# The rest of a quarter of the output weights: a negated copy and an accumulating DMA in place of a subtraction

## The chip, the cores and the metric

One core of one Trainium2 chip runs the kernel. The metric is the device time of one execution in microseconds (us); lower is better.

## What is computed

One layer of a hybrid decoder trunk for 256 tokens of width 4096, in float32. One input projection makes the columns of two head groups (a state-space group and a gated linear recurrence), each group works on its columns, and the two results of 4096 channels each go through one output projection, a residual and a LayerNorm:

```python
proj = x @ w_in                                  # 4096 x 18496
z, xbc, dt_raw, lx, lg = jnp.split(proj, ...)
...                                              # ssd_out and lru_out, 4096 channels each
mix = jnp.concatenate([ssd_out, lru_out], axis=-1)
res = DEEPNORM_ALPHA * x + mix @ w_out           # 8192 x 4096
out = (res - mean) * rsqrt(var + eps) * ln_g + ln_b
```

The change touches only the part `mix @ w_out`, and of the weights only how they are prepared.

## The kernel before, in words

**Three products for one.** Each float32 operand of a projection is split into a high part of 12 significant bits and the rest, both in the matmul's float32r type. The product is high x high + high x rest + rest x high, added up in PSUM.

**The order of the work.** The input projection of the recurrence (LRU) columns comes first, head by head; then the output projection of that half, whose result with alpha*x is spilled to DRAM; then the input projection of the state-space (SSD) columns; then the output projection of the SSD half, with the LayerNorm. All weights stream from DRAM once, in chunks of 128 partitions x 1024 float32 (512 KB).

**The function around the change** is `xstat` (L213 to L232). It makes 512 output columns for both blocks of 128 tokens. It runs over 16 chunks of weights; each chunk holds two of the 32 k-tiles. For a chunk it takes a `raw` tile (one of 4 buffers), loads it with a DMA from the SP queue (L219), calls `split` (L153), and issues 12 matmuls: for each of two k-tiles and two token blocks, high x high (L228), high x rest (L229) and rest x high (L230). `split` takes a `hi` and a `lo` tile (3 buffers each), and does two things:

```python
act.copy(hi, raw)                                # L160, ScalarE
dve.tensor_tensor(out=lo, in0=raw, in1=hi, op=ALU.subtract)   # L161, VectorE
```

So chunk n can be split only when the matmuls of chunk n-3 have let go of their `hi` and `lo`, and the load of chunk n+4 can start only when the split of chunk n has let go of its `raw`.

**Who calls `xstat`.** The output projection of the LRU half calls it 8 times with `src` the mixed activations `mix` (L423 on), the SSD input projection 8 times with `src` the layer's input `X` (the gate columns), and the output projection of the SSD half 7 times with `mix`. The last 512 columns of the SSD half are done by other code (L669 on) that calls `split` itself. The input projection's `wstat` also calls `split`.

**What else stands in the queues.** The elementwise work of a block is written as generators that `tick` advances once for each chunk (L231). In the LRU half, `gen_o1` (L364) loads `xa`, adds alpha*x and stores `spill`, all DMAs on the SP queue. During the last call there (r = 7), `dt_part` (L410) adds 32 matmuls (L419) of a narrow weight. The framework's scheduler then sets the final order on each engine, so instructions can stand earlier or later than they are written. GpSimd (POOL) has next to nothing to do: masks at the start, and small powers and fills (L534, L581, L587) later.

Of the kernel before, what the change touches and what calls it, by code (L numbers as in the profile page):

```python
"""Hybrid SSD / RG-LRU layer with DeepNorm post-norm on one Trainium2 core.

The two projections run on the tensor engine as float32 products made of three
passes: each operand is split exactly into a high part of 12 significant bits
and the rest, both in float32r, and high*high + high*rest + rest*high is
accumulated in float32 in PSUM.

Order: input projection of the LRU columns head by head, output projection of
the LRU half (spilled to DRAM with alpha*x), input projection of the SSD columns
group by group, output projection of the SSD half, LayerNorm.  The elementwise  # L10
work of a block is emitted between the weight chunks of the blocks after it.
"""
# [2 lines left out]

# [4 lines left out]
F32 = mybir.dt.float32  # L20
F32R = mybir.dt.float32r
I32 = mybir.dt.int32
AF = mybir.ActivationFunctionType
ALU = mybir.AluOpType

P = 128
# [5 lines left out]
LAG = 5  # L32
ON_ACT = ((2, 4, 6), (3, 6))
Z0, X0, B0, C0, DT0, LX0, LG0 = 0, 4096, 8192, 9216, 10240, 10304, 14400
# columns of the packed per-channel vectors
LCW, LCB, LBA, LBX, LLAM, SCW, SCB, SNW, MSK, NPK = 0, 128, 160, 192, 224, 256, 448, 496, 528, 534


def body(tc, xT, x, wb, wz, wd, wo, wg, pk, hv, ln_g, ln_b, out):
    nc = tc.nc  # L40
    act, dve, pe, pool, dma = nc.scalar, nc.vector, nc.tensor, nc.gpsimd, nc.sync.dma_start

    stack = contextlib.ExitStack()
    with stack:
        ent = stack.enter_context
        con = ent(tc.tile_pool(name="con", bufs=1))
# [4 lines left out]
        mp = ent(tc.tile_pool(name="mp", bufs=4, space=bass.MemoryType.PSUM))  # L51
        dram = ent(tc.tile_pool(name="dram", bufs=1, space=bass.MemoryType.DRAM))

# [1 line left out]
        pkt = con.tile([P, NPK], F32, name="pkt")  # L55
        hvt = con.tile([P, 3, 64], F32, name="hvt")
        ident = con.tile([P, P], F32, name="ident")
        mler = con.tile([P, P], F32R, name="mler")    # [k, l] = 1 where k <= l
        mgtr = con.tile([P, P], F32R, name="mgtr")    # [k, s] = 1 where k > s
        mle = mler.bitcast(F32)  # L60
        mhalf = con.tile([P, 2], F32, name="mhalf")
        c8 = con.tile([P, 32], F32, name="c8")
# [3 lines left out]
        adl = con.tile([P, 2, 64], F32R, name="adl")  # L66
        dec = con.tile([P, 64], F32, name="dec")
        ea = con.tile([P, 64], F32, name="ea")
        na = con.tile([P, 64], F32, name="na")        # exp(a_log)

        def load_consts():
            dma(pkt, pk)
# [16 lines left out]
            act.copy(mgtr, mgt)  # L89

        def exp_small(dst, src, n):
            """dst = exp(src) to float32 accuracy: 2^k * exp(r / 4)^4, zero below exp(-86.5)."""
            xc, k, r = t2k("ex", [P, n]), t2k("ek", [P, n]), t2k("er", [P, n])
            bits = t2k("eb", [P, n], I32)
            dve.tensor_scalar(xc, src, -87.0, 89.0, op0=ALU.max, op1=ALU.min)
            dve.tensor_scalar(k, xc, math.log2(math.e), 1.5 * 2.0 ** 23, op0=ALU.mult, op1=ALU.add)
            dve.tensor_scalar(k, k, 1.5 * 2.0 ** 23, None, op0=ALU.subtract)
            dve.scalar_tensor_tensor(out=r, in0=k, scalar=-0.693359375, in1=xc, op0=ALU.mult, op1=ALU.add)
            dve.scalar_tensor_tensor(out=r, in0=k, scalar=2.12194440054690583e-4, in1=r, op0=ALU.mult, op1=ALU.add)
            act.activation(r, r, AF.Exp, scale=0.25)  # L100
            yield
            dve.tensor_tensor(out=r, in0=r, in1=r, op=ALU.mult)
            dve.tensor_tensor(out=r, in0=r, in1=r, op=ALU.mult)
            dve.tensor_scalar(bits, k, 126.0, 2.0 ** 23, op0=ALU.add, op1=ALU.mult)
            dve.tensor_tensor(out=r, in0=r, in1=bits.bitcast(F32), op=ALU.mult)
            dve.tensor_scalar(xc, src, -86.5, 2.0, op0=ALU.is_ge, op1=ALU.mult)
            dve.tensor_tensor(out=dst, in0=r, in1=xc, op=ALU.mult)
            yield

        def softplus(dst, src, n, scale):  # L110
            """dst = softplus(scale * src), scale +1 or -1; relative accuracy for all sizes."""
            def t(nm):
                return t2k(nm, [P, n])
            ax, e, z, z2, q = t("ax"), t("e"), t("z"), t("z2"), t("q")
            dve.scalar_tensor_tensor(out=ax, in0=src, scalar=-1.0, in1=src, op0=ALU.mult, op1=ALU.min)
            yield from exp_small(e, ax, n)
            dve.tensor_scalar(z2, e, 2.0, None, op0=ALU.add)
            dve.reciprocal(z, z2)
            dve.tensor_tensor(out=z, in0=z, in1=e, op=ALU.mult)
            yield  # L120
            dve.tensor_tensor(out=z2, in0=z, in1=z, op=ALU.mult)
            dve.tensor_scalar(q, z2, 2.0 / 17, 2.0 / 15, op0=ALU.mult, op1=ALU.add)
            for k in (13, 11, 9, 7, 5, 3, 1):
                dve.tensor_tensor(out=q, in0=q, in1=z2, op=ALU.mult)
                dve.tensor_scalar(q, q, 2.0 / k, None, op0=ALU.add)
            dve.tensor_tensor(out=q, in0=q, in1=z, op=ALU.mult)
            dve.tensor_scalar(ax, src, scale, 0.0, op0=ALU.mult, op1=ALU.max)
            dve.tensor_tensor(out=dst, in0=ax, in1=q, op=ALU.add)
            yield

# [1 line left out]
        pend = []  # L132

        def tick():
# [18 lines left out]
        def split(raw, shape, extra=None):  # L153
# [7 lines left out]
            dve.tensor_tensor(out=lo, in0=raw, in1=hi.bitcast(F32), op=ALU.subtract)  # L161
            return hi, lo

        def rawtile(shape):
            return wp.tile(shape, F32, name="raw", tag="raw", bufs=4)

# [13 lines left out]
                              in1=X[:, k0:k0 + n, 0, :].bitcast(F32), op=ALU.subtract)  # L180

        def wstat(blocks, first=False):
            """Blocks of 256 columns of the input projection, by number, channel-major:
            one PSUM tile [128, 2, (high 256 | rest 256)] per block."""
            accs = [acc.tile([P, 2, 512], F32, name="acc") for _ in blocks]
            k0 = 0
            while k0 < KT:
# [23 lines left out]
            return accs  # L211

        def xstat(src, raws, before=None):  # L213
            """512 columns, sequence-major [128, 2 seq blocks, 512]; raws[chunk] is the DRAM of 2 k-tiles."""
            a = acc.tile([P, 2, 512], F32, name="acc")
            for ch in range(KT // 2):
                k0 = ch * 2
                raw = rawtile([P, 2, 512])
                dma(raw, raws[ch])  # L219
                hi, lo = split(raw, [P, 2, 512])  # L220
                if before is not None:
                    before(k0)
                for k in range(2):
                    kt = k0 + k
                    for sb in range(2):
                        sh = src[:, kt, 0, sb * P:(sb + 1) * P]
                        sl = src[:, kt, 1, sb * P:(sb + 1) * P]
                        pe.matmul(a[:, sb, :], lhsT=sh, rhs=hi[:, k, :], start=(kt == 0), stop=False)  # L228
                        pe.matmul(a[:, sb, :], lhsT=sh, rhs=lo[:, k, :], start=False, stop=False)  # L229
                        pe.matmul(a[:, sb, :], lhsT=sl, rhs=hi[:, k, :], start=False, stop=(kt == KT - 1))  # L230
                tick()  # L231
            return a  # L232
# [9 lines left out]
            return u  # L242

        def conv(u, wbase, bbase, stride, chans):
            """causal conv of width 4 along the free axis; yields between the two tiles."""
            y = t2k("cv")
            for c in range(2):
                ct = chans[c]
# [11 lines left out]
                yield  # L260
            return y

# [1 line left out]
        lgs = {}  # L264

        def gen_lg(h, a):
# [68 lines left out]

        ready = []

# [1 line left out]
        def gen_pre():  # L339
            load_consts()  # L340
            make_masks()
# [16 lines left out]
                a = wstat([lxc])[0]  # L358
            last = start(gen_lx(h, a))

# [1 line left out]
        spill = dram.tile([8, 2, P, 512], F32, name="spill")  # L362

        def gen_o1(r, a):  # L364
# [7 lines left out]
                dma(spill[r, sb], xa[sb])  # L372
                yield

# [1 line left out]
        def gen_dt(a):  # L376
            t = t2k("dtc", [P, S])
            act.copy(t, a[:, 256:512])
# [27 lines left out]
            yield  # L406

        def dt_part(k0, st):
            """columns of dt, [high | rest] of the weight as stationary: rows 0..63 and 64..127 add up."""
            if k0 % 8 == 0:  # L410
                st["raw"] = t2k("dtw", [P, 8, 64])
                dma(st["raw"], wd[k0 // 8])
# [153 lines left out]
            last = start(gen_z(g, a, y))  # L566
        xp_cm.__exit__(None, None, None)

# [1 line left out]
        # out = (res * g) * rstd + (b - mean * rstd * g); the second term is an outer product on the  # L570
        # tensor engine, rows [mh, mh, ml, 1, 1] against [gh, gl, gh, bh, bl]; the columns lie in
        # four row blocks of 32 partitions, one stationary matrix for each.
        fin = ent(tc.tile_pool(name="fin", bufs=1))
        rg = fin.tile([P, 2, D], F32, name="rg")
        R = fin.tile([P, 1024], F32R, name="R")
# [96 lines left out]
        for r in range(8):  # L672
            nx = loads(r)
            wsrc = wo[0, r]
            if r < 7:
                a = xstat(mix, wsrc, before=(lambda k0: flush(last) if k0 >= KT - 4 else None) if r == 0 else None)
                start(gen_o2(r, a, nx))
                if r == 0:
                    start(gen_rows())
        # last 512 columns: the second sequence block follows the first one LAG chunks behind  # L680
        a = [mp.tile([P, 512], F32, name="mp") for _ in range(2)]
        held = {}

# [95 lines left out]
```

## Time and profile before

| | |
|---|---|
| time, median of 2 runs | 2469.82 us (2467.34 to 2472.29) |
| span of the profiled execution, first to last instruction | 2470.1 us |
| TensorE matmuls (PE) busy | 2455.6 us, 99% |
| VectorE (DVE) busy | 1487.8 us, 60% |
| ScalarE (ACT) busy | 1236.2 us, 50% |
| GpSimd (POOL) busy | 9.7 us |
| granted TensorE clock, mean | 0.998 |

The span agrees with the median of the runs to 0.3 us, so times of the trace can be set against the runs directly. A PE that is busy all the time says where the end is set; the shares of the other engines say only how much work they have, not whether PE waits for it. For that one reads PE's idle time by line, and for a single chunk the timeline: when its cast began, when its rest was ready, and when PE first used it.

### The profile page before, as it was taken

To read this page: it belongs to the slowest core of one execution; us is meant where nothing else is said; L and a number is where in the kernel's file an instruction comes from. 1 tells how busy PE (TensorE), PEld (TensorE's weight loads), DVE (VectorE), ACT (ScalarE), POOL (GpSimd) and SP (SyncE) were. 2 spreads that over 40 slices of the span, in tenths; PEclk is the share of its full clock that TensorE was granted. 3 is DMA by queue.
4 is the path that set the end of the run, shared out by engine and by line. 5 is a ranking of instruction groups with operands and counts; after the bars stand their busy time and mean duration, and the time that the engine had idled before them with its cause. 6 is when DMAs were issued, how large, how long until landed. Compare 5 with 4: busy or idle time off the path is not lost.

```text
span 2470.1 us, 32588 instructions
## 1 busy us (share of the span) xinstructions
PE 2455.6 (99%) x12778; PEld 2099.8 (85%) x12778; DVE 1487.8 (60%) x1828; ACT 1236.2 (50%) x1450; POOL 9.7 (0%) x25
## 2 busy tenths in 40 slices
PE   8999999999999999999999999999999999999999
PEld 7888888888888888888888888888888888888887
DVE  6756656666666544546656565656565656655555
ACT  5566556556656433434454454545454444433333
POOL 0000000000000000000000000000000000000000
PEclk9999999999999999999999999999999999999999
DMA  8555655655655766665555555555555555676654
GB/s 278 180 179 185 195 191 173 200 191 171 199 193 181 250 222 208 215 203 185 166 180 171 176 172 178 170 173 175 173 172 177 171 175 172 213 232 204 217 195 172
DMA packets 135898, 471.32 MB, mean 191 GB/s; under 512 B 15504, under 2 KB 16272, under 8 KB 135744
## 3 DMA queue, kind: packets, MB, share of 16 engines
q1 hardware_dynamic: 135744, 469.24, 57.9%
q8 instruction: 100, 1.64, 0.3%
q14 instruction: 54, 0.44, 0.1%
HBM read 460.79 MB, written 8.39 MB: 190 GB/s over the span
## 4 chain that ended last, share of the span: by engine, by line
PE 97%; DMA 1%; DVE 1%; ACT 0%; SPq 0%; issue 0%; ACTq 0%
PE acc L204 32%; PE acc L207 17%; PE acc L230 14%; PE acc L229 14%; PE acc L228 14%; PE mp L507 1%; PE mp L294 1%; PE mp L296 1%; PE mp L295 1%; PE mp L690 1%; PE mp L691 1%; PE mp L689 1%; DMA raw<-in_wb 1%; DMA raw<-in_xT 0%; PE mp L508 0%; PE mp L495 0%
## 5 line engine op out<-in xcount | busy, mean ns | idle before, releaser
L161 DVE TENSOR_TENSOR lo<-raw,hi 128x1024 fp32r<-128x1024 f32 x830 | 1012.3, 1222 | 781.5 <-ACT hi L160 779.5
L160 ACT CAST hi<-raw 128x1024 fp32r<-128x1024 f32 x830 | 870.3, 1050 | 1104.7 <-PE acc L230 552.9
L204 PE MATMUL acc<-X,hi 128*128 128x512 f32 x3584 | 1268.1, 395 | 8.6 <-ACT hi L160 5.7
L207 PE MATMUL acc<-X,lo 128*128 128x256 f32 x3584 | 1015.2, 283 | 0.3 <-DVE lo L161 0.3
L204 PEld LDWEIGHTS acc<-X,hi 128*128 128x128 f32 x3584 | 675.4, 188 | 162.2 <-ACT hi L160 6.0
L207 PEld LDWEIGHTS acc<-X,lo 128*128 128x128 f32 x3584 | 676.2, 189 | 1.1 <-DVE lo L161 0.7
L228 PE MATMUL acc<-hi,mix 128*128 128x512 f32 x960 | 373.7, 389 | 0.0
L229 PE MATMUL acc<-lo,mix 128*128 128x512 f32 x960 | 373.6, 389 | 0.0
L230 PE MATMUL acc<-hi,mix 128*128 128x512 f32 x960 | 373.6, 389 | 0.0
L229 PEld LDWEIGHTS acc<-lo,mix 128*128 128x128 f32 x960 | 180.2, 188 | 37.6
L228 PEld LDWEIGHTS acc<-hi,mix 128*128 128x128 f32 x960 | 180.2, 188 | 37.4
L230 PEld LDWEIGHTS acc<-hi,mix 128*128 128x128 f32 x960 | 180.2, 188 | 37.4
L228 PE MATMUL acc<-hi,X 128*128 128x512 f32 x512 | 207.2, 405 | 0.0
L230 PE MATMUL acc<-hi,X 128*128 128x512 f32 x512 | 202.1, 395 | 0.0
L229 PE MATMUL acc<-lo,X 128*128 128x512 f32 x512 | 202.0, 394 | 0.0
L230 PEld LDWEIGHTS acc<-hi,X 128*128 128x128 f32 x512 | 96.4, 188 | 22.7
L228 PEld LDWEIGHTS acc<-hi,X 128*128 128x128 f32 x512 | 96.4, 188 | 21.9
L229 PEld LDWEIGHTS acc<-lo,X 128*128 128x128 f32 x512 | 96.5, 188 | 21.5
L258 DVE SCALAR_TENSOR_TENSOR cv<-eu,pkt,cv 128x254 f32<-128x254 f32 (+2 forms) x240 | 98.6, 477 | 0.0
L250 ACT ACTIVATE cv<-eu,pkt 128x256 f32<-128x256 f32 x80 | 43.6, 592 | 0.0
L241 DVE TENSOR_TENSOR eu<-acc,elo 128x512 f32<-128x512 f32 x56 | 38.3, 683 | 0.0
L296 PE MATMUL mp<-uh,gl 128*128 128x256 f32 x128 | 36.1, 282 | 0.0
(188 smaller groups left out, 1222.8 us busy)
## 6 DMA issues: line engine op xcount, KB each, us to landing
raw<-in_wb SPq DMA_DIRECT2D x446, 512.0 KB
raw<-in_wo SPq DMA_DIRECT2D x256, 512.0 KB
raw<-in_wz SPq DMA_DIRECT2D x128, 512.0 KB
raw<-in_wg SPq DMA_DIRECT2D x16, 512.0 KB
xa<-in_x SPq DMA_DIRECT2D x16, 256.0 KB
spill<-xa SPq DMA_DIRECT2D x16, 256.0 KB
sp<-spill SPq DMA_DIRECT2D x16, 256.0 KB
out<-rg SPq DMA_DIRECT2D x16, 256.0 KB
```

What stands on the lines that cost most here:

```text
L160: act.copy(hi, raw)
L161: dve.tensor_tensor(out=lo, in0=raw, in1=hi.bitcast(F32), op=ALU.subtract)
L204: pe.matmul(a[:, c, :], lhsT=hi[:, k, sl], rhs=X[:, kt, :, :].rearrange("p a s -> p (a s)"), start=(kt == 0), stop=False)
L207: pe.matmul(a[:, c, 256:512], lhsT=lo[:, k, sl], rhs=X[:, kt, 0, :], start=False, stop=(kt == KT - 1))
L228: pe.matmul(a[:, sb, :], lhsT=sh, rhs=hi[:, k, :], start=(kt == 0), stop=False)
L229: pe.matmul(a[:, sb, :], lhsT=sh, rhs=lo[:, k, :], start=False, stop=False)
L230: pe.matmul(a[:, sb, :], lhsT=sl, rhs=hi[:, k, :], start=False, stop=(kt == KT - 1))
L241: dve.tensor_tensor(out=u, in0=a[:, :, 0:256], in1=lo, op=ALU.add)
L250: act.activation(y[:, c, :], u[:, c, :], AF.Identity, bias=pkt[:, bbase + ct:bbase + ct + 1], scale=w(3))
L258: dve.scalar_tensor_tensor(out=y[:, c, sh:], in0=u[:, c, :S - sh], scalar=pkt[:, o:o + 1], in1=y[:, c, sh:], op0=ALU.mult, op1=ALU.add)
L294: pe.matmul(p[:, j, :], lhsT=gh[:, g, i, sl], rhs=uh[:, i, :], start=(i == 0), stop=False)
L296: pe.matmul(p[:, j, :], lhsT=gl[g][:, i, sl], rhs=uh[:, i, :], start=False, stop=(i == 1))
```

## The change

A second function, `split_add`, stands beside `split`. In `xstat`, and only with `src` the mixed activations, every fourth chunk (2, 6, 10 and 14 of 16) uses it. It makes the same two tiles in three steps: ScalarE's copy to `hi` as before, a second ScalarE instruction that writes minus `hi` to `lo`, and a DMA issued by POOL that adds `raw` to `lo` in place. VectorE has no part in these chunks. Comments and docstrings are blanked elsewhere. The numbers of lines behind the new function are 9 higher.

```diff
+        def split_add(raw, shape):
+
+            hi = wp.tile(shape, F32R, name="hi", tag="hi", bufs=3)
+            lo = wp.tile(shape, F32R, name="lo", tag="lo", bufs=3)
+            act.copy(hi, raw)
+            act.mul(lo, hi.bitcast(F32), -1.0)
+            pool.dma_start(out=lo, in_=raw, accum_op=ALU.add)
+            return hi, lo
...
                 raw = rawtile([P, 2, 512])
                 dma(raw, raws[ch])
-                hi, lo = split(raw, [P, 2, 512])
+                hi, lo = (split_add if src is mix and ch % 4 == 2 else split)(raw, [P, 2, 512])
```

The order changes on the engines with it. First ScalarE, in the first 512 columns of the LRU half, where the last head's result is cast into `mix`. Before:

```order
L322 ACTIVATE th_7382<-th_7382 128x512
L160 CAST hi_7428<-raw_7426 128x1024
L160 CAST hi_7451<-raw_7449 128x1024
L332 CAST mix_89<-hh_7445 128x2x256
L160 CAST hi_7471<-raw_7469 128x1024
L160 CAST hi_7490<-raw_7488 128x1024
```

and in the changed kernel:

```order
L331 ACTIVATE th_7385<-th_7385 128x512
L160 CAST hi_7431<-raw_7429 128x1024
L168 CAST hi_7454<-raw_7452 128x1024
L169 ACTIVATE lo_7455<-hi_7454 128x1024
L341 CAST mix_89<-hh_7448 128x2x256
L160 CAST hi_7475<-raw_7473 128x1024
L160 CAST hi_7494<-raw_7492 128x1024
L160 CAST hi_7516<-raw_7514 128x1024
L168 CAST hi_7536<-raw_7534 128x1024
L169 ACTIVATE lo_7537<-hi_7536 128x1024
```

One chunk in four now has two instructions on ScalarE (L168, L169), one right behind the other; the casts of the other three (L160) stand between them as before.

Next POOL, from the end of the masks on (`rs`, `at`, `G` and `lrs` belong to the norm of the SSD half and to the LayerNorm). Before:

```order
L86 AFFINE_SELECT mgt_541<-mgt_541 128x128
L534 TENSOR_TENSOR rs<-ss,mhalf 128x2 x7
L581 MEMSET at_17714 128x128
L582 MEMSET at_17714 128x4x2
L534 TENSOR_TENSOR rs<-ss,mhalf 128x2
L587 MEMSET G 128x512 x2
L634 TENSOR_TENSOR lrs<-lrs,mhalf 128x1 x2
```

and in the changed kernel, where `lo<-raw` is the accumulating DMA:

```order
L170 DMA lo<-raw 128x1024 x32
L543 TENSOR_TENSOR rs<-ss,mhalf 128x2 x7
L590 MEMSET at_17746 128x128
L591 MEMSET at_17746 128x4x2
L543 TENSOR_TENSOR rs<-ss,mhalf 128x2
L170 DMA lo<-raw 128x1024
L596 MEMSET G 128x512
L170 DMA lo<-raw 128x1024 x2
L596 MEMSET G 128x512
L170 DMA lo<-raw 128x1024 x25
L643 TENSOR_TENSOR lrs<-lrs,mhalf 128x1 x2
```

POOL's queue gets 60 DMAs, 32 in the LRU half and 28 in the SSD half; only the first few of the SSD half have other POOL work between them.

Last PE, where the 32 matmuls of the narrow weight stand (`mp<-X,dts`). Before, at the change from the seventh to the eighth 512 columns of the LRU half:

```order
L230 MATMUL acc_8972<-hi_9253,mix_89 128x512
L419 MATMUL mp_9269<-X_93,dts_9279 128x512 x2
L228 MATMUL acc_9270<-hi_9273,mix_89 128x512
L229 MATMUL acc_9270<-lo_9274,mix_89 128x512
L230 MATMUL acc_9270<-hi_9273,mix_89 128x512
```

and in the changed kernel, in the second 512 columns, at a chunk whose rest comes by the DMA:

```order
L238 MATMUL acc_7792<-lo_7895,mix_89 128x512
L239 MATMUL acc_7792<-hi_7894,mix_89 128x512
L237 MATMUL acc_7792<-hi_7912,mix_89 128x512
L428 MATMUL mp_9297<-X_93,dts_9307 128x512
L238 MATMUL acc_7792<-lo_7913,mix_89 128x512
L239 MATMUL acc_7792<-hi_7912,mix_89 128x512
L237 MATMUL acc_7792<-hi_7912,mix_89 128x512
```

21 of the 32 now stand alone between the first matmul of such a chunk, which needs only `hi`, and the second, which needs `lo`; the other 11 stand in the last call as before. The matmuls of the chunks themselves keep their order.

## Rows read from the trace of the kernel before

**Rows 1.** The page's first part: busy us (share of the span) x instructions.
```profile
PE 2455.6 (99%) x12778; PEld 2099.8 (85%) x12778; DVE 1487.8 (60%) x1828; ACT 1236.2 (50%) x1450; POOL 9.7 (0%) x25
```

**Rows 2.** The page's fourth part: the chain that ended last, by engine.
```profile
PE 97%; DMA 1%; DVE 1%; ACT 0%; SPq 0%; issue 0%; ACTq 0%
```

**Rows 3.** Groups, 800 to 1150 us: busy us, mean ns | idle before, releasers.
```profile
L229 PE MATMUL acc<-lo,mix 128*128 128x512 f32 x480 | 186.8, 389 | 0.0
...
L161 DVE TENSOR_TENSOR lo<-raw,hi 128x1024 fp32r<-128x1024 f32 x126 | 154.1, 1224 | 163.8 <-ACT hi L160 163.8
L160 ACT CAST hi<-raw 128x1024 fp32r<-128x1024 f32 x126 | 132.7, 1053 | 193.8 <-PE acc L230 186.5 <-PE acc L204 7.0 <-ACT er L100 0.2
```

**Rows 4.** Timeline of two chunks in the LRU half: start, length, engine, instruction, [idle].
```profile
900.65 0.39 PE L230 MATMUL acc<-hi,mix 128*128 128x512 f32 x1
...
900.87 0.39 PE L228 MATMUL acc<-hi,mix 128*128 128x512 f32 x1
...
901.07 1.05 ACT L160 CAST hi<-raw 128x1024 fp32r<-128x1024 f32 x1 [1.67 <-PE acc L230]
...
902.16 1.22 DVE L161 TENSOR_TENSOR lo<-raw,hi 128x1024 fp32r<-128x1024 f32 x1 [1.50 <-ACT hi L160]
...
903.59 0.39 PE L228 MATMUL acc<-hi,mix 128*128 128x512 f32 x1
903.79 1.05 ACT L160 CAST hi<-raw 128x1024 fp32r<-128x1024 f32 x1 [1.67 <-PE acc L230]
...
906.31 0.39 PE L228 MATMUL acc<-hi,mix 128*128 128x512 f32 x1
...
906.54 0.39 PE L229 MATMUL acc<-lo,mix 128*128 128x512 f32 x1
```

**Rows 5.** Waits of the SP queue, 800 to 1150 us: total, times, longest.
```profile
SPq L219 <- DVE lo L161: 231.5, 109, 5.7
```

**Rows 6.** Busy time by stretch: PE, PEld, DVE, ACT, POOL, PEclk, DMA share, GB/s.
```profile
800.00:1100.00 300.00, 300.00 (x1326) 248.33 (x1325) 150.77 (x140) 123.74 (x129) 0.00 (x0) 1.00 0.67 219
2160.00:2410.00 250.00, 250.00 (x1104) 207.01 (x1103) 130.07 (x122) 96.95 (x92) 0.00 (x0) 1.00 0.64 212
```

**Rows 7.** Timeline of the SP queue, 995 to 1004 us.
```profile
996.99 0.92 SPq L372 DMA_DIRECT2D spill<-xa  x2
998.72 0.33 SPq L219 DMA_DIRECT2D raw<-in_wo  x1
1002.59 0.33 SPq L412 DMA_DIRECT2D dtw<-in_wd  x1
```

**Rows 8.** Waits of the SP queue, 996 to 1003 us.
```profile
SPq L412 <- DMA spill<-xa: 3.5, 1, 3.5
```

**Rows 9.** Timeline of ScalarE, 1002 to 1006 us.
```profile
1005.28 0.41 ACT L416 CAST dts<-dtw 128x256 fp32r<-128x256 f32 x1 [1.92 <-DMA dtw<-in_wd]
```

**Rows 10.** Timeline of PE around its two longest waits in mid-work.
```profile
9.34 0.49 PE L204 MATMUL acc<-X,hi 128*128 128x512 f32 x1 [1.23 <-ACT hi L160]
...
57.43 0.50 PE L204 MATMUL acc<-X,hi 128*128 128x512 f32 x1 [2.91 <-DVE eu L241]
...
57.88 0.39 PE L204 MATMUL acc<-X,hi 128*128 128x512 f32 x1
...
58.23 0.39 PE L204 MATMUL acc<-X,hi 128*128 128x512 f32 x1
...
58.57 0.61 PE L204 MATMUL acc<-X,hi 128*128 128x512 f32 x1
...
61.76 0.51 PE L204 MATMUL acc<-X,hi 128*128 128x512 f32 x1
```

**Rows 11.** Busy time by stretch behind those two waits (columns as in rows 6).
```profile
12.00:13.00 1.00, 1.00 (x5) 0.81 (x4) 1.00 (x1) 0.75 (x1) 0.00 (x0) 0.50 1.01 414
...
59.00:59.50 0.50, 0.50 (x3) 0.50 (x2) 0.39 (x3) 0.00 (x0) 0.00 (x0) 0.50 1.04 360
...
62.00:63.00 1.00, 1.00 (x7) 0.87 (x7) 0.14 (x1) 1.00 (x2) 0.00 (x0) 1.00 0.05 20
```

## The prediction, made before the changed kernel ran

> **What bounds the kernel now.** I read the busy shares first: PE's matmuls fill 2455.6 of 2470.1 us, the other engines half of it [rows 1]. The chain that ended last says the same from the other end: 97% of it is PE [rows 2]. So only two things can move the time: PE's own work, which the change leaves as it is, and waits of PE. I then asked whether PE waits in the stages that the change touches. The groups of the LRU half show L229, the matmul that reads `lo`, with no idle time before it; VectorE and ScalarE are the ones that wait, VectorE for ScalarE's cast, ScalarE for PE to free a `hi` [rows 3]. By stretch, PE is busy for all 300 us of one half and all 250 us of the other [rows 6]. VectorE's subtraction is thus hidden, and taking it away gains nothing at once. The question is whether what replaces it is also hidden, and for that I need the slack of one chunk.
>
> **The slack of one chunk.** In the timeline [rows 4] the cast of a chunk n starts at 901.07, when the last matmul of chunk n-3 (started at 900.65) has ended. PE begins chunk n-2 at 900.87, n-1 at 903.59 and n at 906.31, so a chunk takes 2.72 us (12 matmuls, 0.227 us from one to the next, though each lasts 0.39). PE first needs the chunk's `lo` at 906.54. With the subtraction, which starts at 902.16 and takes 1.22, `lo` is there at 903.38: 3.2 us early.
>
> **What the change removes.** 60 of the 830 subtractions (4 chunks in each of 8 + 7 calls), 60 x 1.22 = 73 us of VectorE. PE waits for none of them, so: 0.
>
> **What it adds on ScalarE.** 60 instructions over 128x1024 elements. The trace has this size only as the cast, 1.05 us [rows 3]; I take that. The order shows it right behind its cast, so it runs from about 902.1 to 903.2, and the next cast is due at 903.79 [rows 4]: it fits, and nothing else on ScalarE moves. Cost: 0 by itself, but `lo` is not yet `lo`; the DMA can start only at 903.2. The cover left for the DMA, from POOL's issue to landing, is 906.54 - 903.2 = 3.3 us.
>
> **What the DMA takes.** No row shows a DMA issued by POOL, one within SBUF, or one that accumulates, so I bound it by the nearest rows. Below: a load of half the size (256 KB, `dtw`), issued at 1002.59 [rows 7]; the cast that waits for it starts at 1005.28 [rows 9]: 2.7 us. Under that bound the DMA would be hidden. To correct for size, the DMA engines move 219 GB/s at a share of 0.67 [rows 6], which is 327 GB/s at full share, so 256 KB more are 0.8 us and 512 KB are 1.6. At full size that load would be 3.5 us. An accumulation has to read two operands, `raw` and the old `lo`; with the second read, 5.1. Above: a store of 256 KB (`spill`), the second of two that start at 996.99 in 0.92 us, so issued at 997.45 [rows 7]; the SP queue waits for its landing [rows 8] until 1002.59 [rows 7]: 5.1 us. With 0.8 for the size and 1.6 for the second read, 7.5. If reading and writing do not overlap, 1.6 more, 9.1; with about 0.6 for an issue on POOL, 9.7. That is my upper end. I take 6.3, midway between 5.1 and 7.5: it has both a load's reads and a store's confirmed write, and the weight stream keeps the same engines busy for two thirds of the time.
>
> Stall of PE at each such chunk: 6.3 - 3.3 = 3.0 us; at the ends, 0 and 6.4. Stalls do not merge: the next such chunk comes four chunks later, and its cast starts when PE ends the second chunk behind the stall, so every one has the same 3.3 us of cover. Sum: 60 x 3.0 = 180 us.
>
> The Trainium skill, "DMA: Bandwidth & Descriptors", section "Anatomy of one DMA — SWDGE (gpsimd) path", gives 2.0 us plus bytes over 436 GB/s for a DMA from this queue; for 512 KB that is an estimate of 3.2 us, which the 3.3 us of cover would hide. This is the first rival below. "Collectives: The Full Stack" in the Trainium skill, section "The bandwidth ceiling: the fold count and why AG ≠ RS ≠ AR", says that a reducing DMA needs two source reads and so moves at half rate; with it the estimate is 4.4 us, a stall of 1.1 and 2470 + 66 = 2536 us. No run here shows either yet.
>
> **What else a stall sets off.** First, TensorE's clock. After a wait of 2.91 us that ended at 57.43, PE ran at the usual pace for about a microsecond, two matmuls every 0.35 us (57.88 to 58.23); from 58.57 to 61.76 the five pairs took 0.64 each [rows 10], the granted clock was 0.50, the 1.2 GHz level, and was back at 1.00, 2.4 GHz, behind it [rows 11]. That cost 3.19 - 5 x 0.35 = 1.4 us. A shorter wait at the start, 1.23 us [rows 10], was also followed by a clock of 0.50 [rows 11]. So stalls of 3 us are likely to bring this on, not each one surely; I count three in four, 60 x 0.75 x 1.4 = 63 us. Second, the loads. SP issues the load of chunk n+4 when chunk n lets go of `raw`; today that is the end of the subtraction [rows 5], then it will be the landing. The load then has the two chunks after the stall, 5.4 us, before the cast of n+4 needs it, and a load of this size takes about 3.5 (above). Chunks n+5 and n+6 are issued with it and needed 2.7 us later each. Cost 0, with 1.9 us to spare. Third, POOL: what stands between the DMAs at the start of the SSD half are fills and one power, once; 0. Fourth, the order puts 21 of the narrow weight's matmuls into the gap before `lo`; they fill 21 x 0.23 = 5 us of stalls.
>
> **Sum.** 2470.1 (profiled execution, 0.3 above the median) + 180 + 63 - 5 = 2708 us, 9.6% more.
>
> **The rivals.**
> *The DMA is hidden* (not slower). If issue to landing takes 3.3 us or less, and up to 4.1 us where 0.8 x 60 = 49 us stay within 2%, the time is 2470 to 2519. For it: the half-size load at 2.7 us and the full-size one at 3.5. Against it: two reads, a queue that no row shows, and engines shared with the weights. The price turns at a landing 3.3 us behind the second ScalarE instruction.
> *Short stalls, clock unmoved.* A DMA of 4.1 to 5.1 us: stalls of 0.8 to 1.8 us, 2519 to 2578. For it: the corrected load, 5.1, if nothing on POOL adds to it.
> *The accumulation is slow.* Above 8 us, where every pass over the bytes stands one after another: at 9.7 us the stall is 6.4, the clock falls every time, 60 x 7.8 = 468, 2938 us. For it: the store row plus passes. Against it: the engines have a third of their time free [rows 6].
> *Faster.* VectorE's 73 us would have to be on the path; PE shows no idle time behind it [rows 3, 6]. Nothing speaks for it but small shifts of order.
>
> **How the numbers follow.** Forecast (5.1 to 8 us, 2578 to 2836): 0.60. Hidden or nearly: 0.12. Short stalls: 0.12. Slow: 0.14. Faster: 0.02. The range leaves out the hidden case and the far end of the slow one, and reaches from 2530 (stall 1.1, clock unmoved) to 2940. A measurement of this kernel tells about 2%, 49 us, from no change: slower 0.86, same 0.12, faster 0.02.
>
> **What would show it.** Right: in the timeline every fourth chunk's L238 has idle time before it, released by the DMA of `lo`, near 3 us, 60 times, and none at the other chunks; stretches with a granted clock below 1 in the two output halves and nowhere else; SP's waits for `raw` longer, ScalarE with no more idle behind PE than the stalls explain; VectorE 73 us less busy with no effect. Wrong: PE busy throughout as before (hidden); idle time of PE before L237 instead, released by `hi` or by a load of `raw` (then it is the supply of weights and not the rest); or idle time on POOL's or SP's queue behind something other than this DMA.

## The result: 5% slower, and the profile after

The changed kernel took 2597.86 us, median of 2 runs (2596.83 to 2598.9), against 2469.82 before: a ratio of 1.0521, 95% interval 1.0504 to 1.0537, or 128 us more. The forecast was 2708 us, with a range of 2530 to 2940: the direction, the place and the mechanism were right, the size was almost twice what came, 238 us forecast against 128.

The page's first part answers to [rows 1]:

```profile
span 2594.8 us, 32765 instructions
...
PE 2481.1 (96%) x12778; PEld 2099.8 (81%) x12778; DVE 1417.3 (55%) x1768; ACT 1299.3 (50%) x1510; POOL 62.0 (2%) x85
```

VectorE has 70 us less to do (73 were worked out) and ScalarE 63 us more, as worked out; POOL went from 10 to 62 us. PE is busy for 25 us more with the same 12778 matmuls, and the rest of the longer span is idle time. Where that lies is told by the waits of PE over the whole program (us in total, times, longest):

```profile
PE acc L238 <- DMA lo<-raw: 99.7, 58, 5.8
PE acc L213 <- ACT hi L160: 5.2, 2, 4.5
PE acc L213 <- DVE eu L250: 1.8, 1, 1.8
```

L238 is L229 of before, the first matmul that reads `lo`. Before it had no idle time in the LRU half [rows 3], and PE was busy all the time in a stretch of each half [rows 6]; now it has 99.7 us, 58 times of 60, and the releaser named is the accumulating DMA. The other two waits stand at the start of the program, as before. 99.7 us of idle time and 25.5 us of more busy time are 125.2; the span grew by 124.7. So the whole loss is there, if the busy time comes with these waits too, which is worked out below.

One chunk in the timeline, the same place in the program as [rows 4] (start, length, engine, instruction, [idle before]):

```profile
927.11 1.05 ACT L168 CAST hi<-raw 128x1024 fp32r<-128x1024 f32 x1 [1.62 <-PE acc L239]
...
928.20 1.06 ACT L169 ACTIVATE lo<-hi 128x1024 fp32r<-128x1024 f32 x1
...
929.55 0.86 POOL L170 DMA_DIRECT2D lo<-raw  x1 [11.75 <-ACT lo L169]
929.83 1.05 ACT L160 CAST hi<-raw 128x1024 fp32r<-128x1024 f32 x1 [0.57 <-PE acc L239]
...
932.58 0.40 PE L428 MATMUL mp<-X,dts 128*128 128x512 f32 x1
...
934.15 0.50 PE L238 MATMUL acc<-lo,mix 128*128 128x512 f32 x1 [1.18 <-DMA lo<-raw]
```

Follow one chain: cast at 927.11, negation until 929.26, POOL's issue at 929.55, landing at 934.15. From the end of the negation that is 4.9 us. Without the wait, and without the matmul L428 put in there, L238 would have come at 932.58, 3.3 us behind the negation: the cover of the prediction, to the tenth. The narrow weight's matmul L428 fills 0.23 us of the gap, as the order said. The next cast (929.83) keeps its time, and ScalarE's second instruction takes 1.06 us. The view of the DMA gives the transfer itself: its queue (packets, MB, share of 16 engines' span), then the issues (KB each, median us from issue to landing):

```profile
q0 software_dynamic: 8640, 31.46, 6.5%
...
raw<-in_wo SPq DMA_DIRECT2D x256, 512.0 KB, 3.6
...
lo<-raw POOLq DMA_DIRECT2D x60, 512.0 KB, 4.6
```

It lands 4.6 us behind its issue; a load of weights of the same size takes 3.6. The 6.5% of 2594.8 us are 2.8 us of all 16 engines for each accumulation.

**The clock.** Two of the waits were much longer, 5.7 and 5.8 us, in the first 100 us of the LRU half. The first of them on PE, and the granted clock around it beside a usual chunk's (columns as in [rows 6]; a PEclk of 1.00 is 2.4 GHz):

```profile
823.90 0.79 PE L238 MATMUL acc<-lo,mix 128*128 128x512 f32 x1 [5.72 <-DMA lo<-raw]
824.50 0.63 PE L239 MATMUL acc<-hi,mix 128*128 128x512 f32 x1
824.92 0.63 PE L237 MATMUL acc<-hi,mix 128*128 128x512 f32 x1
```

```profile
821.00:822.00 1.00, 0.00 (x0) 0.00 (x0) 0.00 (x0) 0.00 (x0) 0.00 (x0) 0.50 1.00 260
824.00:825.00 1.00, 1.00 (x3) 0.81 (x4) 0.00 (x0) 0.00 (x0) 0.00 (x0) 0.50 0.31 49
934.00:935.00 1.00, 0.85 (x4) 0.72 (x5) 0.85 (x1) 0.00 (x0) 0.00 (x0) 1.00 1.03 418
```

Behind the long wait the matmuls stand 0.43 us apart instead of 0.227, at a granted clock of 0.50, the 1.2 GHz level; behind the usual wait of 1.18 us the clock is 1.00, 2.4 GHz. In the two output halves only five waits were followed by the low clock, those of 5.7, 5.8, 3.3, 2.4 and 2.7 us, with 40 slow matmuls in all: 40 x 0.2 = 8 us. Waits of 2.35, 2.43, 3.25 and 3.41 us were not followed by it, and none of 2.0 us or less was.

**What else PE lost.** A matmul lasts 0.39 us but the next normally starts 0.227 us after it, so each wait leaves a tail of 0.16 us that counts as busy, and the first step behind a wait is 0.34 us (934.15 to 934.49) instead of 0.227. That is 0.27 us for each of 58 waits, 16 us. With the 8 us of the clock it makes 24 of the 25.5.

### The profile page after: what moved, and what is told of

Read it like the earlier page. It is cut to its first block, busy times and chain, and to the rows that moved or that the text cites. A ratio compares the mean times of both kernels' runs of the same rounds, so it can differ in the third digit from the quotient of the medians.

```text
span 2594.8 us, 32765 instructions
## 1 busy us (share of the span) xinstructions
PE 2481.1 (96%) x12778; PEld 2099.8 (81%) x12778; DVE 1417.3 (55%) x1768; ACT 1299.3 (50%) x1510; POOL 62.0 (2%) x85
## 4 chain that ended last, share of the span: by engine, by line
PE 86%; DMA 12%; DVE 1%; ACT 1%; issue 0%; SPq 0%; POOL 0%; ACTq 0%; DVEq 0%; POOLq 0%
PE acc L213 31%; PE acc L216 16%; PE acc L238 11%; DMA lo<-raw 11%; PE acc L239 10%; PE acc L237 10%; PE mp L516 1%; DMA raw<-in_wb 1%; PE mp L305 1%; PE mp L303 1%; PE mp L304 1%; PE mp L700 1%; PE mp L699 1%; PE mp L698 1%; DMA raw<-in_xT 1%
## 5 line engine op out<-in xcount | busy, mean ns | idle before, releaser
L161 DVE TENSOR_TENSOR lo<-raw,hi 128x1024 fp32r<-128x1024 f32 x770 | 939.3, 1223 | 974.9 <-ACT hi L160 972.4
L160 ACT CAST hi<-raw 128x1024 fp32r<-128x1024 f32 x770 | 806.4, 1049 | 1080.1 <-PE acc L239 520.6
L238 PE MATMUL acc<-lo,mix 128*128 128x512 f32 x960 | 384.7, 401 | 99.7 <-DMA lo<-raw 99.7
L239 PE MATMUL acc<-hi,mix 128*128 128x512 f32 x960 | 377.7, 393 | 0.0
L237 PE MATMUL acc<-hi,mix 128*128 128x512 f32 x960 | 377.5, 393 | 0.0
L238 PEld LDWEIGHTS acc<-lo,mix 128*128 128x128 f32 x960 | 182.3, 190 | 161.0 <-DMA lo<-raw 124.5
L238 PE MATMUL acc<-lo,X 128*128 128x512 f32 x512 | 202.0, 394 | 0.0
L238 PEld LDWEIGHTS acc<-lo,X 128*128 128x128 f32 x512 | 96.5, 188 | 21.5
L168 ACT CAST hi<-raw 128x1024 fp32r<-128x1024 f32 x60 | 63.3, 1055 | 96.5 <-PE acc L239 94.7
L267 DVE SCALAR_TENSOR_TENSOR cv<-eu,pkt,cv 128x255 f32<-128x255 f32 (+2 forms) x240 | 98.8, 477 | 0.8 <-ACT cv L259 0.8
L170 POOL DMA_DIRECT2D lo<-raw x60 | 52.1, 868 | 1483.1 <-PE acc L239 782.7
L169 ACT ACTIVATE lo<-hi 128x1024 fp32r<-128x1024 f32 x60 | 63.6, 1060 | 1.8
```

The lines of the kernel that those rows point to most:

```text
L169: act.mul(lo, hi.bitcast(F32), -1.0)
L170: pool.dma_start(out=lo, in_=raw, accum_op=ALU.add)
L267: dve.scalar_tensor_tensor(out=y[:, c, sh:], in0=u[:, c, :S - sh], scalar=pkt[:, o:o + 1], in1=y[:, c, sh:], op0=ALU.mult, op1=ALU.add)
```

## The experiments

The theory: each accumulation costs PE what its landing comes too late, 4.9 us behind the negation against 3.3 of cover, plus the restart. The rivals: the second instruction on ScalarE (S), a fixed cost of POOL's queue rather than the second read (F), and the traffic of the accumulation, which slows the stream of weights whenever it runs (B). The lines shown are of the views of PE's waits and of the DMA issues, with columns as above.

**ScalarE's part alone.** The DMA goes:

```diff
             act.copy(hi, raw)
             act.mul(lo, hi.bitcast(F32), -1.0)
-            pool.dma_start(out=lo, in_=raw, accum_op=ALU.add)
```

> The changed kernel without the accumulating DMA: lo stays minus hi, the rest is left out of a quarter of the chunks. Theory (the DMA lands later than PE needs lo: 4.9 us from the end of ScalarE's second instruction against 3.3 us of cover): no idle time before L238, time 2470 us within 5. Rival S (the second ScalarE instruction delays the casts): 2500 to 2590, with idle time of PE behind ScalarE.

Measured: 2469.03 us, ratio 1.0001 (0.9992 to 1.001). This run leaves out the rest in a quarter of the chunks. PE's waits over the whole run name no DMA and no line of `xstat`. Its first part of the page reads:

```profile
PE 2454.0 (99%) x12778; PEld 2097.6 (85%) x12778; DVE 1416.6 (57%) x1768; ACT 1299.5 (53%) x1510; POOL 9.7 (0%) x25
```

S falls: the 60 negations cost nothing. The same run shows that the 71 us taken off VectorE gain nothing. All of the loss comes with the DMA.

**The same DMA without the second read.**

```diff
-            pool.dma_start(out=lo, in_=raw, accum_op=ALU.add)
+            pool.dma_start(out=lo, in_=raw)
```

> POOL's DMA copies raw to lo instead of adding it (lo is then raw, not the rest): the same issue, bytes written and waits, but one operand read. Theory, with the second read as 1.2 us of the landing (2.8 us of engine time for an accumulation against 1.6 for a weight load of the same size): landing 4.6 to 3.4 us, stall 1.6 to 0.4 us, time about 2500 us (2485 to 2520). Rival F (what is long is POOL's issue and the confirmation of the write, not the second read): landing stays 4.6 us, time about 2595 us.

Measured: 2498.18 us, ratio 1.0125 (1.0109 to 1.0142). PE's waits in this run:

```profile
PE acc L238 <- DMA lo<-raw: 16.7, 14, 3.6
```

Its DMA issues:

```profile
lo<-raw POOLq DMA_DIRECT2D x60, 512.0 KB, 2.9
```

And POOL's own instructions of that line (ns, shortest/median/longest, then the us of the first and the last start):

```profile
L170 POOL DMA_DIRECT2D lo<-raw x60: 527/532/707, 775.0 to 2426.0; - x60
```

The landing fell from 4.6 to 2.9 us, and PE waits 14 times instead of 58. Of the 1.7 us, 0.33 are POOL's own time at the issue (0.86 to 0.53), the rest lies behind it. F falls: the add costs 1.7 us of the landing, and without them the loss is 29 us instead of 128.

**The same accumulation, started 1.06 us earlier.**

```diff
-            act.copy(hi, raw)
-            act.mul(lo, hi.bitcast(F32), -1.0)
+            act.mul(lo, raw, -1.0)
             pool.dma_start(out=lo, in_=raw, accum_op=ALU.add)
+            act.copy(hi, raw)
```

> The same three steps in another order: ScalarE first writes minus the high part of raw to lo (L168), the DMA follows, and the cast to hi comes behind it. The DMA starts 1.06 us earlier and moves the same bytes. Theory (lateness alone): each stall is 1.06 us shorter, 60 x 1.06 = 64 us, time about 2530 us (2515 to 2545). Rival B (the accumulation's traffic slows the stream of weights): about 2595 us as now.

Measured: 2559.86 us, ratio 1.0366 (1.035 to 1.0381): 38 us gained of the 64 expected. PE's waits in this run:

```profile
PE acc L238 <- DMA lo<-raw: 60.7, 41, 4.9
```

Its DMA issues:

```profile
lo<-raw POOLq DMA_DIRECT2D x60, 512.0 KB, 5.2
```

Both sides are partly right. The start does matter, but the median landing is 0.6 us longer than in the changed kernel, which takes back 36 us at most. Why it is longer stays open. The last load of weights is usually issued 1.5 us ahead of the DMA here, in the changed kernel 2.8 us ahead, but that alone does not do it: the accumulation issued at 948.62 had such a load 1.5 us ahead of it (947.10) and landed in 4.4 us. More of them are very late: 14 of 60 landed more than 6 us behind their issue, against 5 in the changed kernel, and at 11 of the 14 a store to `spill` or a load from it was issued between 0.6 us ahead of the DMA and 1.4 us behind it. This was not tried by itself.

**The same accumulation, much earlier.** `lo` of these chunks has its own buffer and is begun one chunk ahead:

```diff
+                if src is mix and ch % 4 == 1:
+                    rawn = rawtile([P, 2, 512])
+                    dma(rawn, raws[ch + 1])
+                    lon = wp.tile([P, 2, 512], F32R, name="loa", tag="loa", bufs=1)
+                    act.mul(lon, rawn, -1.0)
+                    pool.dma_start(out=lon, in_=rawn, accum_op=ALU.add)
...
-            return wk.tile(shape or [P, 2, S], dtype, name=nm, tag="t", bufs=10)
+            return wk.tile(shape or [P, 2, S], dtype, name=nm, tag="t", bufs=8)
```

> The same 60 accumulating DMAs of 512 KB, but lo of these chunks has a buffer of its own (the ring of small tiles is cut from 10 to 8 for it), ScalarE writes minus the high part of raw into it about one chunk earlier, straight from raw, and the cast to hi stays at its place. All bytes move as in the changed kernel; only the time at which the DMA can start differs, by more than 2.7 us. Theory (lateness): the DMA lands before PE needs it, idle time only where it collides with other transfers, time 2470 to 2485 us. Rival B (the accumulation's traffic costs the weight stream): near the 2560 us that the earlier start by 1.06 us alone left, above 2530 us.

Measured: 2492.54 us, ratio 1.0089 (1.0072 to 1.0106). PE's waits in this run:

```profile
PE acc L250 <- DMA loa<-raw: 14.9, 10, 3.4
```

Its DMA issues:

```profile
loa<-raw POOLq DMA_DIRECT2D x60, 512.0 KB, 4.8
```

The same 60 accumulations of 512 KB with a landing no shorter than in the changed kernel cost 22 us instead of 128. B falls as the main cause: five sixths of the loss are lateness. The 22 us, 7 above the upper end expected, are mostly ten waits of up to 3.4 us, at accumulations that landed 6.7 to 9.3 us behind their issue; what delayed these was not tried. The smaller ring of tiles belongs to this run too and was not tried alone.

**Half the bytes, needed later.**

```diff
-            act.mul(lo, hi.bitcast(F32), -1.0)
-            pool.dma_start(out=lo, in_=raw, accum_op=ALU.add)
+            act.mul(lo[:, 1, :], hi[:, 1, :].bitcast(F32), -1.0)
+            pool.dma_start(out=lo[:, 1, :], in_=raw[:, 1, :], accum_op=ALU.add)
+            dve.tensor_tensor(out=lo[:, 0, :], in0=raw[:, 0, :], in1=hi[:, 0, :].bitcast(F32), op=ALU.subtract)
```

> The DMA makes only the second k-tile of the chunk's lo (256 KB); VectorE subtracts the first. Lo's second half is needed six matmuls (1.36 us) later, ScalarE's negation is half as long (0.45 us earlier), and half the bytes land about 1.4 us sooner: cover 5.1 us against about 3.5. Theory: no stall but for collisions with other transfers, time 2470 to 2485 us. Rival B (traffic): half the bytes, half the loss, about 2532 us.

Measured: 2484.32 us, ratio 1.0062 (1.0046 to 1.0078). PE's waits in this run:

```profile
PE acc L239 <- DMA lo<-raw: 11.3, 7, 3.4
```

Its DMA issues:

```profile
lo<-raw POOLq DMA_DIRECT2D x60, 256.0 KB, 3.4
```

At the upper end of what the theory gave, far from B's 2532. If the landing is a fixed part and a part in proportion to size, this and the 4.6 us for 512 KB give them: 1.2 us for each 256 KB, and 2.2 us fixed. Two sizes can't show whether it is.

**Fewer and more of them.** `ch % 4 == 2` becomes `ch % 8 == 2`, and then `ch % 2 == 0`.

> Only chunks 2 and 10 of 16 use the DMA: 30 instead of 60. Theory (each one costs by itself): half of the 128 us, time about 2533 us (2523 to 2543). If stalls hang together, it is clearly off that.

> Every second chunk uses the DMA: 120 instead of 60. Theory with nothing else: twice the 128 us, about 2726 us. Rival B (engines shared): in one period of two chunks the DMA engines then have two loads of 1.6 us and an accumulation of 2.8 us, 6.0 us of work in about 7.0, so transfers meet more often and the landing grows above 5 us: 2750 to 2850 us.

Measured: 2542.40 us with 30 (ratio 1.0291, 1.0275 to 1.0306) and 2693.77 us with 120 (1.0906, 1.089 to 1.0922). Over the 2470.45 us of before, measured beside them, that is 72 us and 223 us: 2.4 us for each accumulation with 30, 2.1 with 60, 1.9 with 120. PE's waits with 30:

```profile
PE acc L238 <- DMA lo<-raw: 52.1, 28, 4.8
```

PE's waits with 120:

```profile
PE acc L238 <- DMA lo<-raw: 157.0, 93, 5.9
```

And its DMA issues:

```profile
lo<-raw POOLq DMA_DIRECT2D x120, 512.0 KB, 5.9
```

With 120 the landing did grow to 5.9 us, as B said, but the time went the other way, below both expectations, since only 93 of 120 accumulations kept PE waiting. The rule of the buffers offers a reason: with such chunks two apart, the cast of chunk n+2 starts when PE ends n-1, which is ahead of the wait for chunk n, so one wait covers part of the next. At four apart it can't. Single chunks bear this out: the DMA issued at 1129.23 landed 7.11 us later and kept PE waiting for only 1.71, where the usual chunk of the changed kernel waits 1.43 for a landing of 4.6. It was not tested by a run of its own. With 30, the time is at the upper end expected and the cost above half by about 8 us; the long waits do not halve with the number: ten were above 2 us with 60, and ten with 30.

**The long waits.** The timeline of the changed kernel, SP's queue before the first of them:

```profile
810.65 0.90 SPq L376 DMA_DIRECT2D xa<-in_x  x2
812.95 0.33 SPq L228 DMA_DIRECT2D raw<-in_wo  x1
813.33 1.41 SPq L376 DMA_DIRECT2D xa<-in_x  x3
817.61 7.07 SPq L228 DMA_DIRECT2D raw<-in_wo  x3
```

Five loads of x and one of weights go out within four microseconds, then POOL's DMA at 815.00, which lands 8.9 us later. The 16 loads of x are left out, so that what stands for x in this run is zero:

```diff
             for sb in range(2):
-                dma(xa[sb], x[r, sb])
+                dve.memset(xa[sb], 0.0)
```

> The changed kernel without the 16 loads of x in the LRU half (xa is set to zero instead, the residual is left out). The longest stalls there, 5.7, 5.8 and 3.3 us, came where several xa loads had been issued in a burst ahead of the accumulation, which then landed up to 9.0 us after its issue. Theory: these stalls fall to the usual 1.2 to 1.4 us, with the low clock behind two of them: 10 to 20 us less, about 2583 us. If the burst is not the cause: 2598 us as now.

Measured: 2591.84 us, ratio 1.0493 (1.0478 to 1.0509), 6 us below the changed kernel; PE's wait for the DMA fell from 99.7 us to this:

```profile
PE acc L238 <- DMA lo<-raw: 91.7, 58, 3.2
```

The two longest waits are gone (1.8 and 3.1 us at their places), so the loads of x made most of them; at the second place two stores to `spill` still go out just ahead. The time fell by 6 us instead of 10 to 20: in this run four waits of 1.8 to 3.1 us in the same half were followed by the low clock, against two in the changed kernel.

## Why the prediction was right, and where its size was off

**What bounds the kernel, and the slack.** Right. PE is the bound, and the cover of 3.3 us was met to the tenth. VectorE's time is worth nothing and ScalarE's second instruction costs nothing: the run without the DMA shows both (1.0001). 58 of 60 accumulations kept PE waiting, at the place that was named and at no other.

**What the DMA takes.** This is the step that was off. The prediction put 6.3 us, midway between a load and a store corrected for the size and the second read, 5.1 and 7.5; it measured 4.9, 0.3 from the end of the negation to the issue and 4.6 to the landing. The lower of the two, the load of `dtw` with 0.8 us for the size and 1.6 for the second read, was right by 0.2 us, in part by luck: its bytes came to 3.2 us and its fixed part to 1.9, and by the fit above the runs give 2.4 and 2.5 (2.2 and the 0.3 before the issue). The second read alone cost 1.7 us, 0.33 of them on POOL. The store of `spill` was the wrong neighbour. Its row was a store behind another store with a load behind it, and it is not what a store takes by itself: the DMA view of the changed kernel has for the stores of the result, of the same size,

```profile
out<-rg SPq DMA_DIRECT2D x16, 256.0 KB, 2.5
```

and with 0.8 and 1.6 that is 4.9, which is what came. (The 2.5 is of the two stores whose landing is known; in the run without the loads of x a store of `spill` itself landed in 2.9.) The 0.6 us for an issue on POOL, at the upper end, had no row; the issue measured 0.86 us.

The usual wait of PE was 1.2 to 1.4 us, the mean with the long ones 99.7 / 58 = 1.7. The prediction's stall is counted from where L238 was due, so the tail of 0.16 us of the matmul before it belongs to it: 99.7 + 58 x 0.16 = 109 us, against 180 less the 5 of the filling. This term was mis-sized by 66 us.

**The page's figure.** By the Trainium skill's "Collectives: The Full Stack", section "The bandwidth ceiling: the fold count and why AG ≠ RS ≠ AR", two reads halve the rate, which the page states for the ReduceScatter of a ring; with the fixed 2.0 us of "DMA: Bandwidth & Descriptors", section "Anatomy of one DMA — SWDGE (gpsimd) path", the estimate was 4.4 us, and this case comes near it: 4.6 measured, by the fit 2.2 fixed and 1.2 for each 256 KB. The second page alone, 3.2 us, is near the plain copy (2.9 us), not the accumulation's 4.6.

**The clock.** 63 us were charged, three stalls in four with the low clock; it was five of 58, 8 us. The chance was taken for stalls of 3 us, from a wait of 2.91 and one of 1.23 at the start of the program; the usual waits were 1.2 to 1.4, and no wait of 2.0 us or less was followed by the low clock in the two output halves of this kernel. So most of this error follows from the first one. Not all of it: of the ten waits above 2 us, five were followed by the low clock.

**What was left out.** The longer first step behind each wait, 0.11 us, 6 us in all. With it the sum closes: 109 + 8 + 6 = 123 of 124.7 us. The filling by the narrow weight's matmuls was there (waits of 1.2 us where the order puts one, 1.4 in the SSD half, where nothing fills).

**The loads and collisions.** That the next loads of weights cost nothing held on the whole: PE has no wait for `hi` or `raw` in these stages. But the prediction took the landing as one number; it spread from 4.4 to 9.0 us, and the longest came where loads of other data went out in a burst just before. At the usual stall of 1.57 us (4.89 less 3.32 in the chunk shown), 60 of them less the filling are 89 us; the late landings add 20.

**The rivals.** Hidden: no, but near, since 1.6 us decided it. Short stalls, clock unmoved, 2519 to 2578: the nearest. The usual DMA of 4.9 us lies in this rival's 4.1 to 5.1, not in the forecast's 5.1 to 8. That the time came into the forecast's 2578 to 2836 all the same is partly luck: the 20 us of late landings, 8 of the clock and 6 of slower first steps lifted it there. Slow accumulation: no. Faster: no.

**The range.** It was said to leave out the far end of the slow case, but its upper end of 2940 takes in that case's 2938. So above the hidden case it excluded next to nothing that had been considered, and that the time fell into it says little.

## What to carry to other kernels

Moving work from an engine that nothing waits for to a DMA replaces a short latency with a long one, so what has to be compared is not the load of the engines but the time from the last input to the first use: here 3.3 us of cover from three buffers, against 4.9 us. The same DMAs begun a chunk earlier, from a buffer of their own, cost a sixth; and nothing could be gained at all, because in these stages no wait of PE had ended with VectorE. For the price of a transfer that the trace does not show, take a row that no other traffic disturbs, correct it for bytes and reads, and count collisions as a term of their own, rather than the middle between a quiet row and a disturbed one.

## What the runs showed of the hardware that was not expected

- An accumulating DMA of 512 KB within SBUF landed 4.6 us behind its issue on POOL, a plain copy of the same tiles 2.9; POOL itself was busy for 0.86 and 0.53 us. From 512 and 256 KB (4.6 and 3.4 us) the accumulation's landing comes to 2.2 us plus 1.2 for each 256 KB.
- The landing of one and the same DMA spread from 4.4 to 9.0 us in one kernel; without the loads of x issued just before, the longest of them was 6.3 us. Its median was 5.2 instead of 4.6 when it started 1.06 us earlier.
- In the changed kernel the low clock followed waits of 2.37, 2.67 and 3.30 us and not others of 2.35, 2.43, 3.25 and 3.41; without the loads of x it followed one of 1.82. The length of the wait alone does not say it.
